# Attention in a hybrid encoder: products with v on 512 columns, and two query blocks per turn of the loop

## The chip, the cores and the metric

The kernel runs on one core of a Trainium2 chip. The metric is the device time of one execution in microseconds (us). Three runs of the kernel before gave 1140.51, 1140.58 and 1142.11 us, median 1140.58. The engines are named as in the profile: PE is TensorE with its matmuls, PEld its weight loads, DVE VectorE, ACT ScalarE, POOL GpSimd.

## What is computed

Two residual layers on 512 tokens of width 1024 in float32: gated linear attention with a gated MLP, then grouped-query softmax attention with a gated MLP. The change lies in the softmax attention, which has 8 query heads in two groups that share a key and a value head, all of width 128:

```python
def attn_mixer(h, w_qkv, q_norm, k_norm, w_out, cos, sin):
    B, S, _ = h.shape
    proj = h @ w_qkv
    q, k, v = jnp.split(proj, [ATTN_Q_HEADS * ATTN_HEAD_DIM,
                               (ATTN_Q_HEADS + ATTN_KV_HEADS) * ATTN_HEAD_DIM], axis=-1)
    ...
    q = apply_rope(rmsnorm(q, q_norm).astype(jnp.float32), cos, sin).astype(h.dtype)
    k = apply_rope(rmsnorm(k, k_norm).astype(jnp.float32), cos, sin).astype(h.dtype)
    ...
    def block(q_blk):
        s = jnp.einsum('bkgqd,bksd->bkgqs', q_blk, k).astype(jnp.float32) * scale
        p = jax.nn.softmax(s, axis=-1).astype(v.dtype)
        return jnp.einsum('bkgqs,bksd->bkgqd', p, v)

    o = lax.map(block, qb)
    o = o.transpose(1, 0, 4, 2, 3, 5).reshape(B, S, ATTN_Q_HEADS * ATTN_HEAD_DIM)
    return o @ w_out
```

## The kernel before

All large products take float32 operands as two parts of the type fp32r: a high part (an ACT copy) and a low part (the DVE difference between the value and its high part). A product is three matmuls: high by high, high by low, low by high (`mm3`, L251). Weights are read by DMA into raw tiles and split in this way just ahead of their use (`Weights`, L103).

The attention (`attention`, L604) works on 32 blocks: 8 heads h by 4 blocks j of 128 queries. The 512 keys are taken in 4 blocks k of 128. One block passes through these functions:

- `scores` (L736): 3 matmuls of 512 columns into a PSUM bank with the tag s (there are two such banks), the maximum over keys (DVE, L745), its scaled negative nb (L746), and the exponential (ACT, L748), which writes the tile p and its row sum.
- `shares` (L751): reciprocal of the sum (DVE, L753) and scaling of p (DVE, L754).
- `turn` (L757): four transposes of 128 by 128 on PE (L766) into a bank with the tag pt (two such banks), and the eviction of the whole bank, 512 columns, into a high and a low tile, pth (ACT, L769) and ptl (DVE, L770). A pair of these tiles holds one half of a head: 4 key blocks by 256 queries.
- `mix` (L772): once per half of a head, 4 key blocks by 3 matmuls of 256 columns into half of the one bank po. After the second half the bank is split (`split`, L669) into oT, the head's attention output as a high and a low part.

The loop (L797) runs over t = 0 to 37. In one turn it issues the scores of block t, then the planned steps of t, then the transposes of block t - 4, the scaling of block t, and, where block t - 6 is the second or fourth of its head, `mix` for that half. The numbers 4 and 6 are `LAGS` (L32). The planned steps are pieces of other work: the projection and rotation of the next pair of heads (`qpair`, L694, by `Q_STEPS` and `Q_READY`, L34) and pieces of the out-projection (`out_steps`, L292, by `O_STEPS`, L37), each piece 6 matmuls of 512 columns (L308). What is left of the out-projection runs behind the loop (L810).

The out-projection ends with `end` (L312): it adds its result to the residual x and calls `chunk` (L217) of the next norm, which writes the high and the low part of a piece of x into a tile with the tag xhl (8 such tiles). The up-projection of the following MLP reads these (L565).

Tiles that are named by `big` (L90) share 22 buffers with the tag g: k, v, q, the rotated values, pth and ptl, and oT of heads 0 to 3. The oT of heads 4 to 7 are taken from the xhl tiles (L782). p is one of 6 tiles with the tag t. An instruction that needs a tile waits until the last reader of its earlier content is done; the framework puts instructions of an engine that don't depend on it ahead, so the order of an engine in the trace isn't always that of the program.

Of the kernel before, what the change touches and what calls it, by code (L numbers as in the profile page):

```python
# [8 lines left out]
F32 = mybir.dt.float32  # L9
F32R = mybir.dt.float32r  # L10
U8 = mybir.dt.uint8
AF = mybir.ActivationFunctionType
ALU = mybir.AluOpType

P = 128
S = 512
D = 1024
KC = D // P
NT = S // P
# [12 lines left out]
LAGS = (4, 6)  # L32
# [14 lines left out]
def hybrid_encoder_kernel(  # L47
# [21 lines left out]
    pe, act, dve, pool, sync = nc.tensor, nc.scalar, nc.vector, nc.gpsimd, nc.sync  # L69
# [8 lines left out]
    def nm(s):  # L78
        uid[0] += 1
        return f"{s}{uid[0]}"  # L80
# [3 lines left out]
    def bank(tag, n):  # L84
        return pp.tile([P, S], F32, tag=tag, bufs=PS[tag], name=nm(n))

    def pair(tag, bufs, dt, n):
        return sp.tile([P, 2 * S], dt, tag=tag, bufs=bufs, name=nm(n))

    def big(dt, n):  # L90
        return pair("g", 22, dt, n)

    def tmp(tag, n, w=S):
        return sp.tile([P, w], F32, tag=tag, bufs={"u": 4, "t": 6, "sq": 3}[tag], name=nm(n))

    def tiny(w, n, tag="tiny"):
        return sp.tile([P, 8], F32, tag=tag, bufs={"tiny": 36, "tiny2": 4}[tag], name=nm(n))[:, :w]
# [76 lines left out]
    two = tmp("u", "two")  # L174
# [76 lines left out]
    def mm3(ps, wh, wl, mh, ml, start, stop):  # L251

        mm(ps, wh, mh, start=start, stop=False)  # L253
        mm(ps, wh, ml, start=False, stop=False)  # L254
        mm(ps, wl, mh, start=False, stop=stop)  # L255
# [348 lines left out]
    def attention(norm, nxt):  # L604
# [64 lines left out]
        def split(y, tile_):  # L669
            act.activation(tile_[:, :S], y, AF.Copy)  # L670
            dve.tensor_tensor(tile_[:, S:], y, tile_[:, :S].bitcast(F32), ALU.subtract)

        def whole(gen):
            while True:
                try:
                    next(gen)
                except StopIteration as e:
                    return e.value
# [15 lines left out]
        def qpair(i, tag="acc"):  # L694
            ys, sc = yield from roped(1 + i, PC_QK, HD ** -0.5, "qsc", tag)
            for e in range(2):
                yield
                t = big(F32R, "q")
                split(ys[e], t)
                heads[2 * i + e] = (t, sc, e)  # L700
# [25 lines left out]
        vh, vl = big(F32R, "vh"), big(F32R, "vl")  # L726
# [6 lines left out]
        oh = [None] * QH  # L733
        probs, pts, pos = {}, {}, {}

        def scores(h, j):  # L736

            qt, sc, e = heads[h]
            kt = kk[h // 4]
            js = slice(j * P, (j + 1) * P)  # L740
            s = bank("s", "s")
            mm3(s, qt[:, js], qt[:, S + j * P : S + (j + 1) * P], kt[:, :S], kt[:, S:], True, True)
            scj = sc[:, 2 * j + e : 2 * j + e + 1]
            mx, nb, sm, rc = (tiny(1, n) for n in ("mx", "nb", "sm", "rc"))
            dve.reduce_max(mx, s, axis=mybir.AxisListType.X)  # L745
            dve.tensor_scalar(nb, mx, scj, -1.0, ALU.mult, ALU.mult)  # L746
            p = tmp("t", "p")
            act.activation(p, s, AF.Exp, scale=scj, bias=nb, accum_out=sm)  # L748
            probs[h, j] = (p, sm, rc)

        def shares(h, j):  # L751
            p, sm, rc = probs[h, j]
            dve.reciprocal(rc, sm)  # L753
            dve.tensor_scalar(p, p, rc, None, ALU.mult)  # L754
            probs[h, j] = p

        def turn(h, j):  # L757

            hf, i = divmod(j, 2)
            if i == 0:  # L760
                pts[h, hf] = tuple(big(F32R, n).rearrange("p (k q) -> p k q", q=256) for n in ("pth", "ptl"))
            ph3, pl3 = pts[h, hf]
            p = probs.pop((h, j))
            tp = bank("pt", "pt")
            for k in range(NT):
                pe.transpose(tp[:, k * P : (k + 1) * P], p[:, k * P : (k + 1) * P], ident)  # L766
            isl = slice(i * P, (i + 1) * P)
            tp3 = tp.rearrange("p (k q) -> p k q", q=P)
            act.activation(ph3[:, :, isl], tp3, AF.Copy)  # L769
            dve.tensor_tensor(pl3[:, :, isl], tp3, ph3[:, :, isl].bitcast(F32), ALU.subtract)  # L770

        def mix(h, hf):  # L772
            ph3, pl3 = pts.pop((h, hf))
            vo = (h // 4) * HD
            if hf == 0:
                pos[h] = bank("po", "po")
            dst = pos[h][:, hf * 256 : (hf + 1) * 256]
            for k in range(NT):
                vsl = slice(k * 256 + vo, k * 256 + vo + HD)
                mm3(dst, vh[:, vsl], vl[:, vsl], ph3[:, k, :], pl3[:, k, :], k == 0, k == NT - 1)  # L780
            if hf == 1:
                t = big(F32R, "oT") if h < 4 else pair("xhl", 8, F32R, "oT")  # L782
                split(pos[h], t)
                oh[h] = (t[:, :S], t[:, S:])

        LAG, LAG2 = LAGS
        blocks = [(h, j) for h in range(QH) for j in range(NT)]
        osteps = out_steps(w_aout, oh, nxt)
        plan = collections.defaultdict(list)
        for i in range(1, QH // 2):  # L790
            g = qpair(i)
# [2 lines left out]
                    plan[first + t] += [g] * n  # L794
        for t in O_STEPS:
            plan[t].append(osteps)
        for t in range(len(blocks) + LAG2):  # L797
            if t < len(blocks):
                scores(*blocks[t])
            for g in plan[t]:  # L800
                next(g, None)
            if LAG <= t < len(blocks) + LAG:
                turn(*blocks[t - LAG])
            if t < len(blocks):
                shares(*blocks[t])
            if t >= LAG2:
                h, j = blocks[t - LAG2]
                if j % 2 == 1:
                    mix(h, j // 2)
        whole(osteps)  # L810

    norms = [Norm(i) for i in range(4)]
    cw = gla(norms[0], norms[1])
    ffn(0, norms[1], cw, norms[2])
    attention(norms[2], norms[3])
    ffn(1, norms[3], cw, None)

# [80 lines left out]
```

## Time and profile before

| | |
|---|---|
| Runs | 1140.51, 1140.58, 1142.11 us |
| Profiled execution: its own time | 1140.29 us |
| Its span, first to last instruction | 1138.6 us |
| Granted TensorE clock | 1.000 |
| PE / DVE / ACT busy | 1130.0 / 688.5 / 481.7 us |
| Transposes (pt), first to last start | 649.1 to 740.6 us, 128 of them |
| Products with v (po) | 192 matmuls of 256 columns |
| Evictions (L769 and L770) | 32 on ACT, 32 on DVE, 512 columns each |

The span is the time from the first to the last instruction of one profiled execution; its own time has the 1.7 us around it as well. In the lines of the groups stand the line of the source, the engine, the operation, the tile that is written and those that are read, partitions by elements, the count, then the busy time in us and the mean ns of one, then the idle time of the engine before them and what ended it. In the timeline the first number is the start, the second the length in us from the first start to the last end of the instructions that a row holds (x4: four of them). Matmuls overlap in their records, so the distance between starts is read, not the length.

### The profile page before, as it was taken

The numbers are of one execution on the slowest core, as the hardware profiler recorded it, in microseconds if no ns is written. First come the engines' busy times: TensorE is split into PE (matmuls) and PEld (weight loads), VectorE is DVE, ScalarE is ACT, GpSimd is POOL, SyncE is SP. The second block draws the span as 40 slices with busy tenths as digits, with TensorE's granted clock in tenths as the row PEclk, the third lists the DMA queues.
The fourth block names the chain that finished last, engine by engine and source line by source line (L and its number), as shares of the span: only waits on it lengthen the run. The fifth ranks groups of instructions, "written<-read, shape, count | busy, mean of one in ns | idle before, by whom it ended". The sixth has DMA issues, their size and how long they took to land. (4 is left out here: it accounts for less than half of the span.)

```text
span 1138.6 us, 13034 instructions
## 1 busy us (share of the span) xinstructions
PE 1130.0 (99%) x5280; PEld 942.2 (83%) x5280; DVE 688.5 (60%) x996; ACT 481.7 (42%) x691; POOL 84.3 (7%) x73
## 2 busy tenths in 40 slices
PE   9999999999999999999999999999999999999998
PEld 8788888888888888888888888888888888888887
DVE  5677654567777777633325689756777777762221
ACT  6465233444444444422234666644444444441210
POOL 0214110000000000000004333000000000000000
PEclk9999999999999999999999999999999999999999
DMA  6322210222323223223247633222232322323320
GB/s 229 139 83 74 77 72 33 79 88 98 111 75 111 98 87 111 80 106 111 74 145 186 151 75 74 56 75 88 97 111 75 111 98 87 111 81 123 130 93 19
DMA packets 19836, 111.66 MB, mean 98 GB/s; under 512 B 2368, under 2 KB 2752, under 8 KB 8256
## 3 DMA queue, kind: packets, MB, share of 16 engines
q1 hardware_dynamic: 17328, 102.42, 25.8%
q0 software_dynamic: 2304, 8.39, 3.8%
q8 instruction: 41, 0.67, 0.2%
q14 instruction: 19, 0.16, 0.0%
q10 hardware_dynamic: 144, 0.02, 0.0%
HBM read 100.34 MB, written 2.10 MB: 90 GB/s over the span
## 5 line engine op out<-in xcount | busy, mean ns | idle before, releaser
L140 ACT ACTIVATE wh<-raw 128x1024 fp32r<-128x1024 f32 x164 | 173.0, 1056 | 337.9 <-PE up L254 132.0
L141 DVE TENSOR_TENSOR wl<-raw,wh 128x1024 fp32r<-128x1024 f32 x164 | 204.0, 1244 | 149.5 <-ACT wh L140 149.1
L253 PE MATMUL up<-xhl,wh 128*128 128x512 f32 x704 | 274.3, 390 | 0.0
L255 PE MATMUL up<-xhl,wl 128*128 128x512 f32 x704 | 274.0, 389 | 0.0
L254 PE MATMUL up<-xhl,wh 128*128 128x512 f32 x704 | 273.9, 389 | 0.0
L253 PEld LDWEIGHTS up<-xhl,wh 128*128 128x128 f32 x704 | 132.2, 188 | 27.5
L255 PEld LDWEIGHTS up<-xhl,wl 128*128 128x128 f32 x704 | 132.1, 188 | 27.4
L254 PEld LDWEIGHTS up<-xhl,wh 128*128 128x128 f32 x704 | 132.2, 188 | 27.2
L255 PE MATMUL dn<-gu,wl 128*128 128x512 f32 x352 | 136.9, 389 | 0.0
L253 PE MATMUL dn<-gu,wh 128*128 128x512 f32 x352 | 136.9, 389 | 0.0
L254 PE MATMUL dn<-gu,wh 128*128 128x512 f32 x352 | 136.9, 389 | 0.0
L576 DVE TENSOR_TENSOR u<-up,R 128x512 f32<-128x512 f32 x88 | 60.4, 688 | 52.3 <-PE up L255 52.2
L578 ACT ACTIVATE y<-u,cw 128x512 f32<-128x512 f32 x88 | 71.2, 812 | 21.7 <-DVE u L576 21.7
L255 PEld LDWEIGHTS dn<-gu,wl 128*128 128x128 f32 x352 | 66.1, 188 | 13.8
L253 PEld LDWEIGHTS dn<-gu,wh 128*128 128x128 f32 x352 | 66.1, 188 | 13.7
L254 PEld LDWEIGHTS dn<-gu,wh 128*128 128x128 f32 x352 | 66.1, 188 | 13.6
L308 PE MATMUL op<-oT,wh 128*128 128x512 f32 x256 | 70.5, 394 | 0.0
L580 DVE SCALAR_TENSOR_TENSOR y<-u,cw,y 128x511 f32<-128x511 f32 x88 | 65.9, 751 | 2.9
L579 DVE SCALAR_TENSOR_TENSOR y<-u,cw,y 128x511 f32<-128x511 f32 x88 | 65.6, 747 | 0.6 <-ACT y L578 0.6
L582 ACT ACTIVATE y<-y 128x512 f32<-128x512 f32 x44 | 27.9, 634 | 88.1 <-DVE y L580 88.0
L308 PEld LDWEIGHTS op<-oT,wh 128*128 128x128 f32 x256 | 47.2, 188 | 9.8 <-ACT p L748 0.3
L281 PE MATMUL vg<-wh,xhl 128*128 128x512 f32 x128 | 50.1, 396 | 0.2 <-ACT wh L140 0.2
(190 smaller groups left out, 1506.8 us busy)
## 6 DMA issues: line engine op xcount, KB each, us to landing
raw<-in_w_up_dram SPq DMA_DIRECT2D x44, 1024.0 KB, 4.8
raw<-in_w_down_dram SPq DMA_DIRECT2D x22, 1024.0 KB, 4.8
wl<-raw POOLq DMA_DIRECT2D x16, 512.0 KB, 4.7
raw<-in_w_vg_dram SPq DMA_DIRECT2D x6, 1024.0 KB, 4.8
raw<-in_w_akq_dram SPq DMA_DIRECT2D x5, 1024.0 KB, 5.1
raw<-in_w_kq_dram SPq DMA_DIRECT2D x4, 1024.0 KB, 4.7
raw<-in_w_gout_dram SPq DMA_DIRECT2D x4, 1024.0 KB, 4.7
raw<-in_w_aout_dram SPq DMA_DIRECT2D x4, 1024.0 KB, 4.7
```

What stands on the lines that cost most here:

```text
L140: act.activation(hi[:, sl], r[:, sl], AF.Copy)
L141: dve.tensor_tensor(lo[:, sl], r[:, sl], hi[:, sl].bitcast(F32), ALU.subtract)
L253: mm(ps, wh, mh, start=start, stop=False)
L254: mm(ps, wh, ml, start=False, stop=False)
L255: mm(ps, wl, mh, start=False, stop=stop)
L281: mm(ps[j][:, :width], xh, wh[:, sl], start=st, stop=False)
L308: mm(pss[ng][n], wt[:, sl], mv, start=k == 0 and i == 0, stop=k == KC - 1 and i == 2)
L576: dve.tensor_tensor(u, ps, norm.R, ALU.mult)
L578: act.activation(y, u, AF.Identity, scale=w(1), bias=w(3))
L579: dve.scalar_tensor_tensor(y[:, 1:], u[:, : S - 1], w(0), y[:, 1:], ALU.mult, ALU.add)
L580: dve.scalar_tensor_tensor(y[:, : S - 1], u[:, 1:], w(2), y[:, : S - 1], ALU.mult, ALU.add)
L582: act.activation(res[1], res[1], AF.Silu)
```

## The change

`turn` makes two pairs of tiles per head instead of one per half: each pair holds 2 key blocks by all 512 queries. The bank of transposes is evicted in two pieces of 256 columns per engine, one into each pair. `mix` runs once per head, on 4 key blocks by 3 matmuls of 512 columns, into the whole bank po. The oT of head 3 also comes from the xhl tiles. The loop takes two blocks per turn: scores of both, planned steps of both, transposes of both, scaling of both, and `mix` in every second turn.

```diff
         def turn(h, j):
 
-            hf, i = divmod(j, 2)
-            if i == 0:
-                pts[h, hf] = tuple(big(F32R, n).rearrange("p (k q) -> p k q", q=256) for n in ("pth", "ptl"))
-            ph3, pl3 = pts[h, hf]
+            if j == 0:
+                pts[h] = [[big(F32R, n).rearrange("p (k q) -> p k q", q=S) for n in ("pth", "ptl")] for _ in range(2)]
             p = probs.pop((h, j))
             tp = bank("pt", "pt")
             for k in range(NT):
                 pe.transpose(tp[:, k * P : (k + 1) * P], p[:, k * P : (k + 1) * P], ident)
-            isl = slice(i * P, (i + 1) * P)
             tp3 = tp.rearrange("p (k q) -> p k q", q=P)
-            act.activation(ph3[:, :, isl], tp3, AF.Copy)
-            dve.tensor_tensor(pl3[:, :, isl], tp3, ph3[:, :, isl].bitcast(F32), ALU.subtract)
-
-        def mix(h, hf):
-            ph3, pl3 = pts.pop((h, hf))
+            js = slice(j * P, (j + 1) * P)
+            for i, (ph3, pl3) in enumerate(pts[h]):
+                ks = slice(2 * i, 2 * i + 2)
+                act.activation(ph3[:, :, js], tp3[:, ks, :], AF.Copy)
+                dve.tensor_tensor(pl3[:, :, js], tp3[:, ks, :], ph3[:, :, js].bitcast(F32), ALU.subtract)
+
+        def mix(h):
             vo = (h // 4) * HD
-            if hf == 0:
-                pos[h] = bank("po", "po")
-            dst = pos[h][:, hf * 256 : (hf + 1) * 256]
+            po = bank("po", "po")
             for k in range(NT):
+                ph3, pl3 = pts[h][k // 2]
                 vsl = slice(k * 256 + vo, k * 256 + vo + HD)
-                mm3(dst, vh[:, vsl], vl[:, vsl], ph3[:, k, :], pl3[:, k, :], k == 0, k == NT - 1)
-            if hf == 1:
-                t = big(F32R, "oT") if h < 4 else pair("xhl", 8, F32R, "oT")
-                split(pos[h], t)
-                oh[h] = (t[:, :S], t[:, S:])
-
-        LAG, LAG2 = LAGS
+                mm3(po, vh[:, vsl], vl[:, vsl], ph3[:, k % 2, :], pl3[:, k % 2, :], k == 0, k == NT - 1)
+            del pts[h]
+            t = big(F32R, "oT") if h < 3 else pair("xhl", 8, F32R, "oT")
+            split(po, t)
+            oh[h] = (t[:, :S], t[:, S:])
+
...
-        for t in range(len(blocks) + LAG2):
-            if t < len(blocks):
-                scores(*blocks[t])
-            for g in plan[t]:
-                next(g, None)
-            if LAG <= t < len(blocks) + LAG:
-                turn(*blocks[t - LAG])
-            if t < len(blocks):
-                shares(*blocks[t])
-            if t >= LAG2:
-                h, j = blocks[t - LAG2]
-                if j % 2 == 1:
-                    mix(h, j // 2)
+        n = len(blocks)
+        for t in range(0, n + LAGS[1], 2):
+            two = (t, t + 1)
+            for b in two:
+                if b < n:
+                    scores(*blocks[b])
+            for b in two:
+                for g in plan[b]:
+                    next(g, None)
+            for b in two:
+                if LAGS[0] <= b < n + LAGS[0]:
+                    turn(*blocks[b - LAGS[0]])
+            for b in two:
+                if b < n:
+                    shares(*blocks[b])
+            h, j = divmod(t + 1 - LAGS[1], NT)
+            if h >= 0 and j == NT - 1:
+                mix(h)
         whole(osteps)
```

## The prediction

> **What bounds the kernel now.** I read the page first, then the windows around the attention loop, then the timeline of TensorE in its quiet end, and last the waits.
>
> ```profile
> span 1138.6 us, 13034 instructions
> PE 1130.0 (99%) x5280; PEld 942.2 (83%) x5280; DVE 688.5 (60%) x996; ACT 481.7 (42%) x691; POOL 84.3 (7%) x73
> ```
>
> TensorE is busy in 99% of the span, so a saving counts only if it shortens TensorE's own sequence or one of its few gaps. The change touches the attention loop alone. The records of its two tiles (shortest/median/longest ns, first and last start) place it: transposes from 649 and products with v up to 746 us, the first scores some microseconds before.
>
> ```profile
> L766 PE MATMUL pt<-ident,p x128: 270/272/309, 649.1 to 740.6; 128*128 128x128 f32 x128
> ...
> L255 PE MATMUL po<-pth,vl x64: 278/283/288, 658.0 to 746.2; 128*128 128x256 f32 x64
> ```
>
> Its windows (busy us of PE, PEld, DVE, ACT and POOL in ten microseconds each):
>
> ```profile
> 650.00:660.00 10.00, 10.00 (x57) 8.53 (x56) 7.68 (x18) 6.79 (x15) 6.74 (x5) 1.00 0.34 76
> ...
> 690.00:700.00 10.00, 9.86 (x62) 8.39 (x61) 8.80 (x22) 7.43 (x16) 0.00 (x0) 1.00 0.57 157
> 700.00:710.00 10.00, 10.00 (x67) 8.84 (x65) 9.63 (x21) 5.73 (x12) 7.92 (x6) 1.00 0.29 54
> 710.00:720.00 10.00, 9.21 (x55) 7.78 (x56) 8.67 (x23) 6.73 (x14) 0.00 (x0) 1.00 0.01 2
> ...
> 740.00:750.00 10.00, 10.00 (x59) 8.73 (x59) 3.88 (x6) 3.32 (x5) 0.00 (x0) 1.00 0.01 2
> ```
>
> TensorE is full in most of the loop, at a granted clock of 1.00. VectorE is nearly full from 690 to 720 (8.67 to 9.63 of 10) and idle by more than half from 740. So in the middle a second engine stands close behind TensorE, and at the end TensorE is alone. What TensorE waited for between 645 and 748 us (total us, times, longest):
>
> ```profile
> ACT p L748 <- DVE nb L746: 13.0, 14, 2.6
> ...
> DVE rc L753 <- ACT p L748: 10.7, 16, 1.4
> ...
> PEld s L253 <- ACT p L748: 2.3, 5, 1.0
> ...
> PE s L253 <- ACT p L748: 0.8, 1, 0.8
> ...
> PEld op L308 <- ACT p L748: 0.3, 1, 0.3
> ...
> PEld po L254 <- DVE ptl L770: 0.3, 1, 0.3
> ```
>
> The weight loads waited 2.3 + 0.3 + 0.3 = 2.9 us for softmax work (the 0.8 us of the matmul is part of the same wait). That is the whole stall that this change can remove, about 0.25% of the span; the rest of TensorE's time is its own work.
>
> **The change, part by part.** *Products with v.* Per head 24 matmuls of 256 columns become 12 of 512. The end of the loop shows both widths side by side, undisturbed:
>
> ```profile
> 738.81 1.18 PE L308 MATMUL op<-oT,wh 128*128 128x512 f32 x4
> 739.82 0.62 PE L308 MATMUL op<-oT,wl 128*128 128x512 f32 x2
> 740.28 0.60 PE L766 MATMUL pt<-ident,p 128*128 128x128 f32 x4
> 740.64 0.36 PE L253 MATMUL po<-pth,vh 128*128 128x256 f32 x1
> 740.84 0.28 PE L254 MATMUL po<-ptl,vh 128*128 128x256 f32 x1
> 740.96 0.28 PE L255 MATMUL po<-pth,vl 128*128 128x256 f32 x1
> ...
> 744.89 0.28 PE L253 MATMUL po<-pth,vh 128*128 128x256 f32 x1
> ...
> 746.21 0.28 PE L255 MATMUL po<-pth,vl 128*128 128x256 f32 x1
> 746.33 1.09 PE L308 MATMUL op<-oT,wh 128*128 128x512 f32 x4
> ...
> 747.71 1.07 PE L308 MATMUL op<-oT,wh 128*128 128x512 f32 x4
> ...
> 749.07 1.07 PE L308 MATMUL op<-oT,wh 128*128 128x512 f32 x4
> ```
>
> What matters is the distance from start to start. Twelve of 256 columns run from 744.89 to 746.33: 1.44 us, 0.120 each. Six of 512 columns run from 747.71 to 749.07: 1.36 us, 0.227 each. So a 512-column product is worth 0.24 us of the old form and costs 0.227: per head 24 x 0.120 - 12 x 0.227 = 0.16 us, over 8 heads 1.3 us. That is the upper bound. The lower one comes from 512-column products in the crowded part, the scores of one block:
>
> ```profile
> 659.18 0.40 PE L253 MATMUL s<-k,q 128*128 128x512 f32 x1
> 659.41 0.40 PE L254 MATMUL s<-k,q 128*128 128x512 f32 x1
> 659.65 0.39 PE L255 MATMUL s<-k,q 128*128 128x512 f32 x1
> 659.88 0.40 PE L253 MATMUL B<-xhl,wh 128*128 128x512 f32 x1
> ```
>
> Three take 0.70 us, 0.233 each, and the saving is 24 x 0.120 - 12 x 0.233 = 0.08 us a head, 0.6 us in all. Most heads lie in the crowded part and some in the quiet one; I take the middle, 0.9 us. The 96 weight loads that go are worth nothing more: the start-to-start distance already holds them.
>
> [...]
>
> *Transposes of two blocks together.* The question is what a switch costs. The four transposes at 740.28 take 0.36 us to the next start, and the product after them takes 0.20 instead of 0.12, so 0.44 in all. Within the group the four last 0.60 together; one alone lasts 0.27 (the median above), so the fourth starts 0.33 us after the first and they are 0.11 apart. Four times 0.11 is 0.44: nothing is left for the switch. The same rows bound it: from nothing to the 0.08 us of that first product, times 16 switches saved, so 0 to 1.3 us. I take zero, since the spacing within the group already explains the total.
>
> *Evictions.* Per block one ACT copy and one DVE subtract of 512 columns become two each of 256, as the k blocks now go to two pairs of tiles. Durations over the whole run (count | busy us, mean ns):
>
> ```profile
> L769 ACT ACTIVATE pth<-pt 128x512 fp32r<-128x512 f32 x32 | 19.0, 592 | 12.9 <-PE pt L766 12.7
> ...
> L501 ACT ACTIVATE sa<-kv 128x256 f32<-128x256 f32 x8 | 3.1, 384 | 11.4 <-PE kv L500 11.4
> ```
> ```profile
> L770 DVE TENSOR_TENSOR ptl<-pt,pth 128x512 fp32r<-128x512 f32 x32 | 21.9, 685 | 5.1 <-ACT pth L769 5.0
> ...
> L423 DVE TENSOR_TENSOR ga<-ga,t 128x256 f32<-128x256 f32 x8 | 3.4, 419 | 0.0
> ```
>
> ACT: 2 x 384 - 592 = 176 ns more a block, 5.6 us over 32. DVE: 2 x 419 - 685 = 153 ns more, 4.9 us over 32. All of it lies beside TensorE's work as long as that does not wait; without the cover it is worth up to 4.9 us, since the two engines work at the same time.
>
> *The order of a turn.* Scores of two blocks, then the planned steps, then eight transposes, the two scalings, and every second turn one product with v of 12 matmuls, about 2.7 us. The two s banks are asked for at once, but each is the one used two blocks before, as now. ACT gets two exponentials in a row while DVE does the other block's maximum, so part of the 13.0 and 10.7 us in which ACT and DVE stood waiting for one another should close. DVE thus gains slack and loses 4.9 us of it; how this leaves TensorE's 2.9 us of stalls no row says. The bounds are all gone (-2.9) and the whole eviction cost exposed (+4.9). I take unchanged: both effects act on the same queue, with opposite signs.
>
> *Tiles.* The eight pth/ptl tiles of two heads can be alive at once where four were, which by counting the live tiles stays within the 22 of tag g. Head 3's oT moves into the xhl ring, so norm 3's chunk 3 must wait for the last reader of that oT. The rows of chunk 4 show what that looks like:
>
> ```profile
> 768.11 1.07 PE L308 MATMUL op<-oT,wh 128*128 128x512 f32 x4
> ...
> 769.67 0.73 ACT L220 ACTIVATE xhl<-x,prm 128x512 fp32r<-128x512 f32 x1 [0.75 <-PE op L308]
> ```
> ```profile
> 775.59 0.39 PE L253 MATMUL up<-xhl,wh 128*128 128x512 f32 x1
> ```
>
> Chunk 4 was written just after the step of oT 4 (768.11 to 769.47). Chunk 3 would follow oT 3's step, one step earlier at about 768.1; its 0.73 us on ACT and about the same on DVE end near 770, and the matmul that reads it first stands at 775.59. Cost zero, 5 us of cover; without it, at most the 1.5 us of those two instructions.
>
> **The sum** against the profiled execution, 1138.6 us of span and 1.7 around it, 1140.29: -0.9 (products), 0 (transposes, stalls, chunk 3), so 1139.4. The median of the runs stands 0.3 above the profiled one, so I forecast 1139.7 us, which a measurement hardly tells from no change: for this kernel I count 0.2%, 2.3 us, as the least that it can tell.
>
> **The rivals.** *Faster: the pairs also remove the stalls.* With two exponentials in flight, s banks come free before TensorE asks. All of the 2.9 us goes: 1140.6 - 0.9 - 2.9 = 1136.8. For it speaks that the waits name p, and that DVE's biggest idle time is on p too. Against it, TensorE's own emptiest window (9.21 of 10 from 710 to 720) follows the one where DVE is fullest, so some of the stall is DVE's load and not the order.
>
> *Slower: DVE becomes the bound of the middle.* From 690 to 720 DVE has 30 - 27.1 = 2.9 us free; its part of the extra subtracts, some 12 blocks at 153 ns, takes 1.8 of them, and in 700 to 710 more than is there. In its queue the maximum of the next block stands behind four subtracts, each behind an ACT copy; the exponential waits for the maximum and TensorE for the bank. It decides once TensorE has no planned step to put in between. At the price of the whole eviction cost the time is 1140.6 - 0.9 + 4.9 = 1144.6. Against it: the chain of softmax ends early, and TensorE has out-projection steps to run meanwhile:
>
> ```profile
> 732.85 0.49 DVE L754 TENSOR_SCALAR p<-p,rc 128x512 f32<-128x512 f32 x1
> ```
>
> This is the last scaling, and the last transposes start at 740.28, 7 us later.
>
> [...]
>
> *It doesn't do what it says for TensorE:* the 512-column products keep 0.24 us, if both operands fresh from ACT and DVE slow the stream. Then nothing is saved: 1140.6. The scores, of the same kind, show 0.233, which speaks against it.
>
> **How the numbers follow.** The forecast has 0.34, the last rival 0.06; both are within 0.2% (0.40). Stalls gone or nearly so, 0.28, is faster by over 0.2% (below 1138.3). DVE as the bound, 0.32, is slower (above 1142.9); it gets a little more than its opposite because the extra 10 us of ACT and DVE work is certain and the smoother queue only argued. The likeliest case alone would lie from 1138.3 to 1142.9. The range reaches to both outer cases, 1136.5 to 1145.0.
>
> **What would show it.** Right: 96 po matmuls of 512 columns, 0.227 to 0.235 apart; transposes in eights, still 0.11 apart; 64 evictions on each engine of about 384 and 419 ns; waits of PE and PEld for p of about 2.9 us; the last po about 1 us earlier. The faster rival: those waits below 1 us, the DVE wait for p well below 10.7. The slower one: waits of PE for p or ptl above 5 us, DVE above 9.5 in 690 to 720. The forecast fails if a switch to transposes has a price that the rows hide, or if the stage after the loop waits for chunk 3.

## The result, and the profile after

The changed kernel took 1145.10 us (median of 7 runs, 1143.79 to 1145.84) against 1140.63 before (7 runs): 4.5 us slower, ratio 1.0034 with a 95% interval from 1.0024 to 1.0044. Forecast were 1139.7 us as the likeliest and 1136.5 to 1145.0 as the range. The profiled execution took 1143.79 us, with a span of 1142.1, so the two profiles are 3.5 us apart; where the other microsecond of the median may come from is taken up under the last experiment.

First the ends of the attention part in the timelines of PE, the first score and the first product of the up-projection. Before:

```profile
630.70 0.40 PE L253 MATMUL s<-k,q 128*128 128x512 f32 x1
...
773.55 0.39 PE L253 MATMUL up<-xhl,wh 128*128 128x512 f32 x1
```

After:

```profile
631.07 0.40 PE L253 MATMUL s<-k,q 128*128 128x512 f32 x1
...
777.09 0.39 PE L253 MATMUL up<-xhl,wh 128*128 128x512 f32 x1
```

From one to the other it was 142.85 us, and is 146.02: 3.17 of the 3.5 us lie in this part, called the attention part below. Next the windows of the changed kernel (busy us of PE, PEld, DVE, ACT and POOL):

```profile
650.00:660.00 10.00, 9.32 (x48) 7.08 (x46) 8.64 (x16) 4.38 (x12) 6.68 (x5) 1.00 0.31 70
660.00:670.00 10.00, 9.28 (x45) 7.76 (x46) 9.03 (x25) 7.20 (x17) 0.92 (x1) 1.00 0.33 59
...
680.00:690.00 10.00, 9.09 (x44) 7.08 (x43) 9.33 (x20) 7.51 (x18) 2.29 (x2) 1.00 0.28 54
690.00:700.00 10.00, 10.00 (x54) 8.46 (x53) 8.37 (x23) 6.03 (x16) 0.87 (x1) 1.00 0.59 157
700.00:710.00 10.00, 9.82 (x51) 7.69 (x49) 8.11 (x23) 6.56 (x16) 5.65 (x5) 1.00 0.28 52
710.00:720.00 10.00, 7.75 (x41) 6.24 (x42) 10.00 (x26) 6.16 (x16) 2.04 (x2) 1.00 0.01 2
```

TensorE, which lacked 0.8 us from 710 to 720, now lacks 2.25, and 0.7 to 0.9 in three windows that were full or nearly so. DVE has no idle time left from 710 to 720. The waits of the changed kernel between 640 and 760 us (total us, times, longest) name a new one:

```profile
ACT pth L769 <- DVE ptl L770: 9.1, 8, 2.5
...
PEld s L253 <- ACT p L748: 4.6, 8, 1.2
...
PEld pt L764 <- issue: 3.3, 3, 1.9
...
PE pt L764 <- DVE ptl L770: 2.4, 2, 1.7
```

ACT, between two copies of the same bank, waits 9.1 us for DVE's subtracts. Before, that wait didn't exist. TensorE's wait for p has grown from 2.3 us to 4.6, and it waits for the transposes' banks too. The longest gap in the timeline of the changed kernel shows how:

```profile
708.61 0.41 DVE L770 TENSOR_TENSOR ptl<-pt,pth 128x256 fp32r<-128x256 f32 x1
...
709.05 0.38 ACT L769 ACTIVATE pth<-pt 128x256 fp32r<-128x256 f32 x1 [1.63 <-DVE ptl L770]
...
709.44 2.67 POOL L664 TENSOR_TENSOR ry<-rt,rt 64x512 f32<-64x512 f32 x2
709.65 0.74 DVE L770 TENSOR_TENSOR ptl<-pt,pth 128x256 fp32r<-128x256 f32 x2
710.32 2.08 DVE L754 TENSOR_SCALAR p<-p,rc 128x512 f32<-128x512 f32 x2
710.54 0.63 PE L764 MATMUL pt<-ident,p 128*128 128x128 f32 x4 [0.72 <-DVE ptl L770]
710.73 0.63 ACT L670 ACTIVATE q<-ry 128x512 fp32r<-128x512 f32 x1 [1.30 <-POOL ry L664]
711.27 0.36 ACT L769 ACTIVATE pth<-pt 128x256 fp32r<-128x256 f32 x1
...
712.32 0.41 DVE L770 TENSOR_TENSOR ptl<-pt,pth 128x256 fp32r<-128x256 f32 x1
...
712.87 0.63 PE L764 MATMUL pt<-ident,p 128*128 128x128 f32 x4 [1.71 <-DVE ptl L770]
```

To read it: these are the two banks of one turn; which row belongs to which follows from the order of the program and from what released each row. In the first bank, the second copy starts only at the end of that bank's first subtract (709.05 after 708.61 + 0.41). Its own subtract is one of the two at 709.65, and the next four transposes, at 710.54, waited 0.72 us for it. In the second bank, the first subtract is the other one at 709.65. The second copy comes at 711.27, behind a copy of q (710.73) for which ACT had waited 1.30 us, until POOL had rotated it. The second subtract then stands behind two scalings (710.32), which take 1.04 us each where the usual one takes 0.48. The bank comes free with it at 712.73, and the transposes that need the bank start at 712.87, after 1.71 us without work for TensorE. So one bank makes two round trips between ACT and DVE instead of one, each behind whatever these engines have in their queues.

### The profile page after: what moved, and what is told of

Same layout as the page of the kernel before. It is cut to its first block, busy times and chain, and to the rows that moved or that the text cites. A ratio compares the mean times of both kernels' runs of the same rounds, so it can differ in the third digit from the quotient of the medians.

```text
span 1142.1 us, 12929 instructions
## 1 busy us (share of the span) xinstructions
PE 1129.4 (99%) x5184; PEld 936.9 (82%) x5184; DVE 696.3 (61%) x1028; ACT 485.1 (42%) x723; POOL 84.0 (7%) x73
## 4 chain that ended last, share of the span: by engine, by line
PE 94%; DVE 3%; ACT 1%; DMA 0%; POOL 0%; issue 0%; SPq 0%; POOLq 0%; ACTq 0%
PE up L254 14%; PE up L253 14%; PE up L255 14%; PE op L308 8%; PE dn L253 7%; PE dn L254 7%; PE dn L255 7%; PE vg L282 2%; PE vg L283 2%; PE vg L281 2%; PE o L521 2%; PE kv L500 1%; PE pt L764 1%; DVE p L754 1%; PE B L253 1%; PE B L254 1%
```

## The experiments

The theories: **E**, the evictions in two pieces cost it, either by the alternation on one bank (E1) or by the additional instructions (E2); **P**, the pairing of two blocks costs it; later **M**, that the products with v come late, in a single run per head, and **G**, that this run is too long in one piece. All kernels stand against runs of the kernel before on the same chip (1140.4 to 1140.5 us).

**Two blocks per turn alone** (`pairs_only`): `turn` and `mix` of before in the loop of after. The end of the loop, against the changed kernel:

```diff
...
             h, j = divmod(t + 1 - LAGS[1], NT)
-            if h >= 0 and j == NT - 1:
-                mix(h)
+            if 0 <= h < QH:
+                mix(h, j // 2)
```

> Theory E (the evictions in two pieces per engine cost it: more DVE work, and the second ACT copy of a bank behind the first DVE subtract): with two blocks per turn but whole-bank evictions and products of 256 columns as before, about the time of before, 1140.6 +- 1. Theory P (the pairing costs it: both pt banks asked for at once, two scalings in a row): slower by 4 us or more, 1144.6 or above, with stalls of about 6 us in the loop.

Measured 1140.58 us, ratio 1.0001 (0.9992 to 1.0010). The pairing costs nothing, and it gains nothing: P falls.

**Everything but the pairing** (`mix512_single`): `turn` and `mix` of after in the loop of before, one block a turn. The end of the loop, against the kernel before:

```diff
...
-                if j % 2 == 1:
-                    mix(h, j // 2)
+                if j == NT - 1:
+                    mix(h)
```

> One block per turn as before, but evictions in two pieces and products of 512 columns. Theory E: slower than before by about 4 us, 1144 to 1146. Theory P: the products' saving alone, 1139.7.

1145.48 us, ratio 1.0053 (1.0039 to 1.0067). The loss is in these two functions. Of the five executions three took 1145.4 to 1145.5 us at a granted clock of 1.000, and two, at 0.999 and 0.998, took 1147.2 and 1148.7.

**Copies first** (`copies_first`): in the changed kernel, both copies of a bank ahead of both subtracts.

```diff
             for i, (ph3, pl3) in enumerate(pts[h]):
-                ks = slice(2 * i, 2 * i + 2)
-                act.activation(ph3[:, :, js], tp3[:, ks, :], AF.Copy)
-                dve.tensor_tensor(pl3[:, :, js], tp3[:, ks, :], ph3[:, :, js].bitcast(F32), ALU.subtract)
+                act.activation(ph3[:, :, js], tp3[:, 2 * i : 2 * i + 2, :], AF.Copy)
+            for i, (ph3, pl3) in enumerate(pts[h]):
+                dve.tensor_tensor(pl3[:, :, js], tp3[:, 2 * i : 2 * i + 2, :], ph3[:, :, js].bitcast(F32), ALU.subtract)
```

> The changed kernel with both ACT copies of a bank issued ahead of both DVE subtracts. If the alternation on the bank is what costs (theory E, first half): the 9.1 us of ACT waiting for ptl are gone and the time is 1140 to 1142. If the extra DVE work costs (theory E, second half) or the pairing (theory P): no gain, about 1145.

1142.35 us, ratio 1.0016 (1.0007 to 1.0025): a little slower than E1 had it, and 2.7 us of the 4.5 are back with the same instructions in another order. ACT's wait for ptl, 9.1 us in the changed kernel, is gone. In the profiled executions the gain is smaller: the attention part takes 144.71 us instead of 146.02.

**The eviction alone, in the kernel before.** Three kernels change nothing else: copy, subtract, copy, subtract on two key blocks each (`only_alternating`); copy, copy, subtract, subtract (`only_copies_first`); one whole copy and two subtracts (`only_subtracts`). The edit of the first:

```diff
-            act.activation(ph3[:, :, isl], tp3, AF.Copy)
-            dve.tensor_tensor(pl3[:, :, isl], tp3, ph3[:, :, isl].bitcast(F32), ALU.subtract)
+            for ks in (slice(0, 2), slice(2, 4)):
+                act.activation(ph3[:, ks, isl], tp3[:, ks, :], AF.Copy)
+                dve.tensor_tensor(pl3[:, ks, isl], tp3[:, ks, :], ph3[:, ks, isl].bitcast(F32), ALU.subtract)
```

> The kernel before with nothing changed but the eviction: copy, subtract, copy, subtract on 2 key blocks each. Theory E, now in two halves (E1: the second copy waits for the first subtract; E2: the additional instructions on ACT and DVE): 4 to 6 us slower, 1145 to 1146, with ACT waits for ptl. Rival M (one late product with v per head, at the coarser grain, is what stands out in the one-block loop): about 1140.5.

> The same with both copies ahead of both subtracts. E1: 1141 to 1142, most of the loss gone. E2: as with the alternating order, 1145. Rival M: 1140.5.

> The kernel before with one whole ACT copy and the subtract in two pieces: additional work on DVE alone, 153 ns a block, 4.9 us in all. E1: 1140.5. E2 if DVE is the engine that matters: 2 to 5 us slower.

| | median, us | ratio, interval |
|---|---|---|
| `only_alternating` | 1144.05 | 1.0029 (1.0019 to 1.0039) |
| `only_copies_first` | 1141.18 | 1.0006 (0.9997 to 1.0014) |
| `only_subtracts` | 1140.32 | 0.9997 (0.9988 to 1.0006) |

The alternation alone makes 3.5 us. The same 64 copies and 64 subtracts in the other order make 0.7, which the interval doesn't tell from nothing, and the additional DVE work alone makes none. E1 holds and E2 falls; M, which had forecast 1140.5 us for the first, falls as the only cause. In `only_alternating` the two pieces share one tile pth as well as the bank. In the changed kernel each piece has a tile of its own and the wait is there too (9.1 us), so what is left as the ground of the order is the bank. The copies of `only_alternating` (count | busy us, mean ns | idle time ahead of them and what ended it):

```profile
L770 ACT ACTIVATE pth<-pt 128x256 fp32r<-128x256 f32 x64 | 23.1, 382 | 18.8 <-PE pt L766 10.9 <-DVE ptl L771 7.8
```

And those of `only_copies_first`:

```profile
L770 ACT ACTIVATE pth<-pt 128x256 fp32r<-128x256 f32 x64 | 21.8, 383 | 14.8 <-PE pt L766 14.6
```

The copies last the same, 382 and 383 ns; the 7.8 us behind DVE are in one kernel alone.

**Taking two banks in turn** (`interleaved`): in the changed kernel, copy and subtract for the first half of each of the two banks, then for the second halves (`evict` holds one copy and one subtract).

```diff
...
+            if LAGS[0] <= t < n + LAGS[0]:
+                got = [turn(*blocks[b - LAGS[0]]) for b in two]
+                for i in range(2):
+                    for g in got:
+                        evict(blocks[t - LAGS[0]][0], i, *g)
```

> The changed kernel with the same 64 copies and 64 subtracts, each second copy of a bank still behind that bank's first subtract, but the two banks of a turn taken alternately, so that the other bank's copy lies between. E1 (ACT stands still in the alternation): 1142 to 1143, near copies_first. If the dependence itself made the loss however it is covered: 1145.

1143.68 us, ratio 1.0027 (1.0017 to 1.0038), not near `copies_first`. ACT's wait for ptl fell only from 9.1 us to 8.1, and the gaps stand where they stood, since the second round trip is still there and still ends behind the two scalings. So this run doesn't tell ACT's standing still from the late bank, and a cover of the wait was not got in this way.

**Whole evictions with products of 512 columns** (`whole_bank`): the eight transposes of a turn go into the two banks by key half, so a bank holds 2 key blocks by 256 queries and is evicted whole.

```diff
...
             for i, (ph3, pl3) in enumerate(pts[h]):
...
+                tp = bank("pt", "pt")
+                for k in range(2):
+                    for b in range(2):
+                        o, c = (2 * k + b) * P, (2 * i + k) * P
+                        pe.transpose(tp[:, o : o + P], ps[b][:, c : c + P], ident)
+                tp3 = tp.rearrange("p (k q) -> p k q", q=2 * P)
+                act.activation(ph3[:, :, js], tp3, AF.Copy)
+                dve.tensor_tensor(pl3[:, :, js], tp3, ph3[:, :, js].bitcast(F32), ALU.subtract)
```

> The changed kernel with the eight transposes of two blocks sorted by key half, so that each bank holds 2 key blocks by 256 queries and is evicted whole (32 copies and 32 subtracts of 512 columns). Theory E: stalls as before, minus 0.9 for the products, about 1139.7. Theory P: still about 1145.

1141.40 us, ratio 1.0007 (0.9998 to 1.0016): 3.7 of the 4.5 us are back, but 1.7 us are missing to E's 1139.7. So there is a second cause. Three experiments look for it.

**The grain of the products** (`whole_halves`): in `whole_bank`, the products of the first two key blocks in one turn, those of the last two in the next.

```diff
...
+            h, j = divmod(t - 1 - LAGS[1], NT)
+            if h >= 0 and j == NT - 1:
+                mix(h, 1)
...
-            if h >= 0 and j == NT - 1:
-                mix(h)
+            if h >= 0 and j == NT - 1 and h < QH:
+                mix(h, 0)
```

> The version with banks sorted by key half, the 12 products of a head split into 6 in one turn (first two key blocks) and 6 in the next. Theory G (the grain: one long run of products per head leaves TensorE without other work between scores in the turns that have none): the 1.8 us that whole_bank lost against its saving come back, 1139.6 to 1140.2. If the grain doesn't matter: 1141.4.

1142.23 us (1140.63 to 1143.14), ratio 1.0011 (1.0003 to 1.0020). G falls as a forecast, but its eleven executions are of two kinds. Four at a granted clock of 1.000 took 1140.63 to 1141.06 us, less than any of `whole_bank` (1141.20 to 1141.75); seven at 0.999 or 0.998 took 1141.98 to 1143.14. The profiled one is of the first kind, and its attention part takes 143.22 us where that of `whole_bank` takes 143.86. So at the full clock the cut gains about 0.6 us, a third of what G expected, and in most executions a lower clock seems to take more than that away (see the last section).

**Late products alone** (`pairs_late`): `pairs_only` with both halves of a head in the turn of the second. **Sorted banks alone** (`pairs_sorted`): `pairs_only` with the banks by key half.

```diff
-            if 0 <= h < QH:
-                mix(h, j // 2)
+            if 0 <= h < QH and j == NT - 1:
+                mix(h, 0)
+                mix(h, 1)
```

> pairs_only with both halves' products (24 of 256 columns) issued together in the turn of the second half. If the late run of products is what costs whole_bank its 1.8 us: about 1142.3. If not: 1140.6.

> pairs_only with the transposes of two blocks sorted by key half, whole evictions, products of 256 columns per half head. If the sorted banks cost whole_bank its 1.8 us: about 1142.3. If not: 1140.6.

`pairs_late` took 1143.73 us, ratio 1.0027 (1.0017 to 1.0037); `pairs_sorted` 1140.88, ratio 1.0004 (0.9995 to 1.0013). Sorting is free, and the lateness is the second cause. It seems to cost more here than expected, but the profile of `pairs_late` holds a stretch at half clock that is worth 1.7 us (see the last section); its attention part of 146.26 us without these 1.7 is 1.4 longer than the 143.11 of `pairs_only`. Rows of `pairs_late` (DVE and PE):

```profile
707.83 2.56 DVE L754 TENSOR_SCALAR p<-p,rc 128x512 f32<-128x512 f32 x2
710.31 0.68 DVE L671 TENSOR_TENSOR oT<-po,oT 128x512 fp32r<-128x512 f32 x1
710.91 0.20 DVE L746 TENSOR_SCALAR nb<-mx,qsc 128x1 f32<-128x1 f32 x1
```
```profile
709.23 0.71 PE L308 MATMUL op<-oT,wh 128*128 128x512 f32 x2
712.07 0.50 PE L253 MATMUL s<-k,q 128*128 128x512 f32 x1 [2.12 <-ACT p L748]
```

The two slow scalings and the split of oT hold back nb, so the exponential and then the bank are late, and TensorE has nothing to do for 2.1 us. In `pairs_only` the same place has a half head's products in it:

```profile
708.81 1.04 PE L766 MATMUL pt<-ident,p 128*128 128x128 f32 x8
...
709.60 0.36 PE L253 MATMUL po<-pth,vh 128*128 128x256 f32 x1
...
711.12 0.40 PE L253 MATMUL s<-k,q 128*128 128x512 f32 x1
```

**Half of the scalings on ACT**, in three kernels: `whole_bank_act`, `whole_halves_act` and `pairs_act`.

```diff
-            dve.tensor_scalar(p, p, rc, None, ALU.mult)
+            if j % 2 == 0:
+                dve.tensor_scalar(p, p, rc, None, ALU.mult)
+            else:
+                act.activation(p, p, AF.Copy, scale=rc)
```

> The version with banks sorted by key half, with the scaling of every second block on ACT instead of DVE. If DVE's queue is what leaves 4.4 us of stalls there: stalls below 3 us and 1139 to 1140. If not (ACT is in front of the s banks as well): 1141.4 or more.

> The same with the scaling of every second block on ACT. Theory G and the DVE queue add up: 1138.5 to 1139. If both cure the same stalls: 1139.4 as whole_bank_act.

> Two blocks per turn, products of 256 columns and whole evictions as in pairs_only, with the scaling of every second block on ACT. If the gain of whole_bank_act over whole_bank (1.95 us) is the relief of DVE's queue and not bound to the wide products: 1139 to 1140. If it only mends what the wide products broke: 1140.6.

| | median, us | ratio, interval |
|---|---|---|
| `whole_bank_act` | 1139.45 | 0.9991 (0.9982 to 0.9999) |
| `whole_halves_act` | 1139.29 | 0.9990 (0.9981 to 0.9998) |
| `pairs_act` | 1139.53 | 0.9994 (0.9985 to 1.0003) |

The window of the loop in `whole_bank`, then in `whole_bank_act`:

```profile
640.00:735.00 95.00, 91.89 (x463) 74.36 (x462) 81.70 (x184) 61.22 (x119) 26.84 (x22) 1.00 0.35 87
```
```profile
640.00:735.00 95.00, 92.96 (x475) 76.12 (x474) 74.28 (x171) 71.28 (x136) 26.61 (x22) 1.00 0.35 86
```

DVE goes from 81.7 to 74.3 us, ACT from 61.2 to 71.3, and TensorE is busy 1.1 us longer in the same 95. These are the fastest versions, about 1 us below the kernel before; the intervals of the first two end just below 1, and that of `pairs_act` reaches over it. The attention parts of the three profiles agree on the size: 141.88, 141.51 and 141.63 us against 142.85 before. `pairs_act` gets nearly all of it with products of 256 columns, so the relief of DVE is what gains, and what the wide products add, 0.1 to 0.2 us, lies within the intervals. `whole_halves_act` is no faster than `whole_bank_act`, so the cut of the products and the relief of DVE cure the same stalls.

**The attention part of each profile**, from the first score to the first product of the up-projection. It leaves out the start of the kernel, where executions differ for a reason of their own (next experiment); in three further profiles of the changed kernel it was 145.96, 145.96 and 145.95 us.

| | attention part, us | against before |
|---|---|---|
| before | 142.85 | |
| changed kernel | 146.02 | 3.17 |
| `pairs_only` | 143.11 | 0.26 |
| `pairs_sorted` | 143.13 | 0.28 |
| `only_alternating` | 145.92 | 3.07 |
| `only_copies_first` | 143.46 | 0.61 |
| `copies_first` | 144.71 | 1.86 |
| `whole_bank` | 143.86 | 1.01 |
| `whole_halves` | 143.22 | 0.37 |
| `pairs_late`, with 1.7 us lost to half clock | 146.26 | 3.41 |
| `pairs_act` | 141.63 | -1.22 |

**The changed kernel, three further profiles.**

> The changed kernel again, for its profile. If a halved clock behind TensorE's gap near 711 us makes the difference between its runs: a time above 1144.5 comes with 3.4 us of clock 0.5 from about 712.5 us, a time near 1143.8 without. If something else does: no such stretch in the slower ones.

> The changed kernel, second look: as in the first, a time above 1144.5 with a stretch of half clock near 712.5 us, or one near 1143.8 without; slower and without it speaks for something else.

> The changed kernel, third look: as in the first, a time above 1144.5 with a stretch of half clock near 712.5 us, or one near 1143.8 without; slower and without it speaks for something else.

They took 1143.16, 1145.85 and 1143.42 us, none with a halved clock in the loop. The one of 1145.85 lost its time at the start of the kernel: its first score stands at 633.16 us, that of the profiled execution of 1143.79 us at 631.07. From 5 to 10 us it ran 11 matmuls, the other 17. First the longer one, then the other:

```profile
5.00:10.00 5.00, 4.25 (x11) 3.34 (x11) 3.48 (x6) 3.69 (x7) 0.00 (x0) 1.00 0.97 354
```
```profile
5.00:10.00 5.00, 4.25 (x17) 3.16 (x18) 3.87 (x7) 4.22 (x8) 0.00 (x0) 1.00 0.97 346
```

The rows of TensorE in these windows, in the same order:

```profile
8.09 0.63 PE L283 MATMUL vg<-wh,xhl 128*128 128x512 f32 x1
8.51 0.63 PE L282 MATMUL vg<-wl,xhl 128*128 128x512 f32 x1
```
```profile
8.08 0.39 PE L282 MATMUL vg<-wl,xhl 128*128 128x512 f32 x1
8.31 0.40 PE L283 MATMUL vg<-wh,xhl 128*128 128x512 f32 x1
```

The same products are 0.42 us apart in the one and 0.23 in the other, nearly twice as far, although both windows list a clock of 1.00. `interleaved` shows the same distance in a window that lists a clock of 0.50 (two scores at 715.21 and 715.64). So the opening matmuls of the longer execution ran at about half speed, up to 10.65 us, from where they are 0.22 to 0.28 apart.

So 2 us of difference between these executions come from a place that the change doesn't touch. The kernel before has longer executions too (1142.11 among its runs, 1142.57 in the one run beside these three). The changed kernel's median lies 1.3 us above its profiled execution for a second reason, as it seems: of its seven runs, 1144.67, 1145.10 (the median) and 1145.36 us list a granted clock of 0.998, while the profiled one lists 1.000. A stretch at half clock as in the last section is the likely cause, since the profile of `interleaved` has one and lists 0.998 as well; but these three were not profiled, so it isn't shown.

## Why the prediction was wrong, point by point

**Products with v: right, also in size.** From the quiet end of the loop of the changed kernel:

```profile
743.56 1.03 PE L764 MATMUL pt<-ident,p 128*128 128x128 f32 x8
744.35 0.94 PE L308 MATMUL op<-oT,wh 128*128 128x512 f32 x3
```
```profile
747.17 0.39 PE L253 MATMUL po<-pth,vh 128*128 128x512 f32 x1
...
749.66 0.39 PE L255 MATMUL po<-pth,vl 128*128 128x512 f32 x1
749.89 1.07 PE L308 MATMUL op<-oT,wh 128*128 128x512 f32 x4
```

Twelve take 2.72 us, 0.227 each, as the out-projection's rows had said. In the crowded part they are 0.23 to 0.24 apart, as the scores had said:

```profile
705.78 0.40 PE L253 MATMUL po<-pth,vh 128*128 128x512 f32 x1
706.02 0.39 PE L254 MATMUL po<-ptl,vh 128*128 128x512 f32 x1
706.25 0.40 PE L255 MATMUL po<-pth,vl 128*128 128x512 f32 x1
706.48 0.39 PE L253 MATMUL s<-k,q 128*128 128x512 f32 x1
```

**Transposes together: right.** Eight take 0.79 us to the next start; with the 0.08 us that the product behind them is late, as before, it is 0.11 each. A switch costs nothing that could be saved.

**Chunk 3: right.** It moved behind the last reader of oT 3, as forecast, and TensorE goes from the out-projection to the first product of the up-projection (777.09) without a gap.

**Evictions: the step that failed.** The durations were right (foreseen 384 and 419 ns), in the groups of the changed kernel:

```profile
L770 DVE TENSOR_TENSOR ptl<-pt,pth 128x256 fp32r<-128x256 f32 x64 | 25.4, 417 | 3.6 <-ACT pth L769 2.6
L769 ACT ACTIVATE pth<-pt 128x256 fp32r<-128x256 f32 x64 | 23.1, 385 | 19.1 <-PE pt L764 9.7 <-DVE ptl L770 9.1
```

But the prediction counted them as work and bounded them by their length, "beside TensorE's work as long as that does not wait", and its sum put the term at 0. It didn't follow the order within a bank. Both engines read the same bank, and the program makes the second copy wait for the first subtract, though it needs nothing of it: in the rows above, the copy starts after the subtract of the same bank has ended (709.05 after 709.02), and these waits of ACT make 9.1 us between 640 and 760. `only_alternating` puts 3.5 us on this, and `only_subtracts` shows that the subtract's added length by itself is free (1140.32 us, ratio 0.9997). Why the reads of one bank are put in an order isn't shown; what the prediction should have followed is which read of a bank stands behind which.

**"The order of a turn": the second step that failed.** It looked at scores, scalings and banks and left out that the products of a head's first half move back by a turn. Before, they were the work that TensorE had while softmax was late. `pairs_late` shows what their absence costs: 3.3 us, of which some 1.7 are the half clock that followed the gap in its profile. Stalls were taken as unchanged because two effects of opposite sign were seen. One half of the first effect did come: between 640 and 760 us DVE's wait for p (L753) is 2.5 us in `pairs_only` and 0.5 in the changed kernel, where it was 12.1. ACT's wait for nb (L748) did not close by the pairing: 15.5 us in `pairs_only`, where it was 14.6. And the pairing gains no time by itself.

**The balance.** The attention part grew by 3.17 us. With 0.9 us saved in the products, an estimate from the distances above, TensorE's stalls there grew by about 4.1 us, more than the 2.9 us that the prediction had counted as all there was.

**The rivals.** The slower one named a time, 1144.6, that was 0.5 us off, and that it came so near is luck in part: its price, the length of the additional subtracts, is not what costs (`only_subtracts`). Its picture of DVE's queue, with subtracts that each stand behind a copy, was nearer to what happened than the forecast's. Of its signs, waits above 5 us came (4.6 for p and 2.4 for ptl), and DVE above 9.5 only from 710 to 720. Its remark that the score chain ends 7 us early, and so could slip, was no help, since the gaps lie in the middle: there TensorE took up out-projection products again only behind the transposes that it waited for. The faster rival is refuted for this version; about 1 us of the 2.9 that it hoped for came when DVE was relieved of half the scalings. The range missed by 0.1 us, at the end that belonged to the slower rival.

**What stays open.** Alternation and lateness were each shown alone. How they share the 4.1 us in the changed kernel follows only from single profiles: `whole_bank`, which takes away the alternation and has no lower clock in its profile, is 2.2 us shorter in the attention part than the changed kernel, and 1.9 are left to the kernel before less the 0.9 of the products. That fits the 1.4 us that the lateness costs in `pairs_late` at the full clock, but no run takes away the lateness alone. The share of the half clock in the changed kernel's median isn't shown either.

## What to carry to other kernels

The eviction that two engines share was priced here by its round trips between their queues, not by its instructions: the same 64 copies and 64 subtracts cost 3.5 us in turn and, with the copies first, 0.7, which the interval doesn't tell from nothing. When one must be cut, let one engine finish the bank before the other starts. A wider product that has to wait for more of its input moves back in the program (1.4 us in `pairs_late`, without the half clock); ask what the engine did in its place. And where one engine's queue is nearly full (DVE, busy 81.7 of 95 us in `whole_bank`), try moving some of its work to another: here half of the scalings on ACT were worth about 1 us against the kernel before, as much as the saving on the engine that is the bound, at the edge of what the runs tell.

## What the runs showed that was not expected

In two profiles a gap of TensorE of about 2 us (2.12 and 1.70) was followed by a stretch at half clock. In `pairs_late`, the windows behind its wait of 2.12 us (the number behind POOL's is the granted clock):

```profile
710.00:712.00 2.00, 0.00 (x0) 0.00 (x0) 2.00 (x5) 0.85 (x3) 0.11 (x1) 1.00 0.00 0
712.00:714.00 2.00, 1.93 (x6) 1.55 (x7) 1.97 (x7) 2.00 (x6) 0.00 (x0) 0.68 0.00 0
714.00:716.00 2.00, 2.00 (x7) 1.49 (x6) 2.00 (x5) 0.27 (x1) 0.00 (x0) 0.50 0.00 0
716.00:718.00 2.00, 2.00 (x17) 1.83 (x16) 1.41 (x4) 1.30 (x3) 0.00 (x0) 0.97 0.00 0
```

The clock was short by 2 x 0.32 + 2 x 0.50 + 2 x 0.03 = 1.7 us of full speed (1.7 / 0.50 = 3.4 us at half clock), which is about half of what `pairs_late` lost in that profile. `interleaved` shows the same stretch behind its gap of 1.70 us (0.66, 0.50 and 0.99 from 712 to 718, again 1.7 us); the changed kernel, with the same gap (1.71 us in its first profile), shows it in none of four profiles, and `whole_halves`, with a wait of 1.9 us in front of a score, lists a clock of 1.000 in its one. But three runs of the changed kernel (0.998) and most of `whole_halves` (0.999 or 0.998) were longer and list a lower clock. So a gap of this length cost its own time and, in the two profiles that show the stretch, 1.7 us more. What decides whether the stretch follows isn't shown.

The scaling of p took 1.04 to 1.28 us instead of 0.48 in two places where POOL's rotation ran beside it (710.32 in the changed kernel, with the rotation from 709.44 to 712.11, and 707.83 in `pairs_late`, where POOL was busy 4.78 of the 5 us up to 710). That is part of what made the subtract at 712.32 and, in `pairs_late`, nb so late.
